# A three-block network on one core: statistics, blocks and one attention pair taken at other steps of the phase borders

## The chip, the core and the metric

The kernel runs on one core of one Trainium2 chip. The metric is the device time of one execution in microseconds: 2200.09 us is the median of three runs (2199.76 to 2200.43).

## What is computed

A sequence of 512 tokens of width 1024 goes through three mixers, each followed by a gated feed-forward network. All data is float32.

```python
# block 1: modulated (sh, sc, g come from a condition vector)
u = rms_norm(x, mix_pre_g) * (1 + sc1) + sh1
x = x + g1 * rms_norm(mix(u) @ w_out, mix_post_g)      # mix: mLSTM and a gated convolution
u = rms_norm(x, ffn_pre_g) * (1 + sc2) + sh2           # the "modulated norm"
x = x + g2 * rms_norm(ffn_conv(u), ffn_post_g)
# blocks 2 and 3: attention with forget gates ("fox"), a gated linear recurrence ("hgrn")
for mixer in (fox, hgrn):
    h = h + rmsnorm(mixer(rmsnorm(h, g0)), g1)
    h = h + rmsnorm(swiglu(rmsnorm(h, g2)), g3)
```

Five borders concern the change: the modulated norm (before the first network), and four plain ones (before fox, before the second network, before hgrn, before the third network). At each of them a projection ends, its output is normalised and added to the residual `X`, and the sum, normalised again, is the input `U` of the next phase.

## The kernel before

**Layout.** Everything lies transposed: 128 of the 1024 features on the partitions, 512 tokens along a row, so `X`, `U` and the projection's output `out.y` have 8 blocks (`KB`) each. The tokens fall into two halves of 256. A product of two float32 values is made of three: each operand is split into a high and a low part, and `mm3` (line 427) issues high by high, high by low and low by high, lines 430 to 432 of the profile. A weight unit's high part is a cast on ScalarE (line 155), its low part a subtraction on VectorE (line 157), both from `Weights.split`.

**Steps.** TensorE's order is the program's. Between products the program calls `slot()` (line 389), one *step*: it first runs evacuations that were posted and have waited out their lag, then resumes every generator in `sides` once (`rate` 1.0 at these borders). So a generator's `yield` says behind how many further products its next TensorE instruction stands. ScalarE, VectorE and GpSimd get their order from the compiler, which ranks by place in the program and by what is ready. Each engine then works through its own queue in that order. The last argument of a generator's `chain`, `hf`, is the half.

**A border.** `tail` (line 503; `tail_all`, line 518, at the modulated norm) computes the projection's last columns, first for the first half of the tokens, then for the second, and after each half appends `nxt.chain(out, hf)` to the sides. A chain takes the column sums of the squares over the partitions: `rms` (line 578) has four products with ones (line 562), a scaling on VectorE (line 584), a power on GpSimd (`rpow`, line 567); then `bcast` (line 570) lays the result along the partitions by two transposes (line 575).

- `Norm.chain` (line 218) then makes one block a step: `block` (line 236) updates `X` (`residual`, lines 1159 and 1160), writes the high and low parts of `U` (243, 244) and adds the new square (593, 594). When a half's eight blocks are made, `upto` (line 229) starts `pre` (line 249): its sums, and one step later its broadcast and a copy into `box["rb"]` (line 256). `U` is not yet multiplied by that second factor; each evacuation of the next phase multiplies by `rb`.
- `ModNorm.chain` (line 282) makes one residual block a step, waits three steps, takes the second sums, and copies their broadcast into `self.rb` (line 304). The blocks are normalised in `get` (line 307; lines 314, 319 and 320), two ahead of the product that needs them.

**The next phase.** `group_halves` (line 477) opens it: six accumulators at the networks and at hgrn, four (and the gate rows, `extra`) at fox; first all eight blocks of the first half of the tokens, then of the second. It calls `norm.get` for each block and a step after every 18 products (15 at fox), eight steps a half. The first four accumulators are the four banks of `mm`, the others lie in `ax` (four banks too). It ends with `norm.finish()` and posts the evacuations (line 1177 in a network, 1510 at hgrn). Then come full `unit`s of 24 products, one `mm` bank each; at fox `unit_tok`, whose first two token blocks lie in `ax`.

**Fox.** `fox_gate` leaves the cumulated gate rows in `self.C` (line 1338); the scores of a pair of heads need them (line 1370). `fox_pair` (line 1341) waits until its keys and `C` are there, then four more steps for pair 0 and two for the others. At most two sides run at once.

Of the kernel before, what the change touches and what calls it, by code (L numbers as in the profile page):

```python
# [19 lines left out]
KB = 8  # L20
# [189 lines left out]
class Norm:  # L210
# [6 lines left out]

    def chain(self, out, hf):
        k = self.k
        yield  # L220
        r = out.r(hf)
        yield
        self.out = out
        self.rb[hf] = k.bcast(r)
        while self.n[hf] < KB:
            yield
            self.upto(self.n[hf] + 1, hf)

    def upto(self, n, hf):
        while self.n[hf] < min(n, KB):  # L230
            self.block(self.n[hf], hf)
            self.n[hf] += 1
            if self.n[hf] == KB:
                self.k.sides.append(self.pre(hf))
# [24 lines left out]
    def get(self, kb, hf):  # L259
        k = self.k  # L260
        while hf not in self.rb:
            k.slot()
        self.upto(kb + 2, hf)
        return self.U[kb]
# [8 lines left out]
class ModNorm:  # L273
# [7 lines left out]

    def chain(self, out, hf):
        k, c = self.k, HALVES[hf]
        yield
        r = out.r(hf)
        yield
        rb = k.bcast(r)
        if self.ss is None:
            self.ss = k.blk("ss")
        for j in range(KB):  # L290
            x = k.X[j][:, c]
            k.residual(x, out.y[j][:, c], rb, self.g[:, j:j + 1])
            if j == KB - 1:
                last = k.tmp(shape=[128, 256])
                k.nc.scalar.activation(last, x, AF.Square)
            else:
                k.square_acc(self.ss[:, c], x, j == 0)
            yield
        for _ in range(3):
            yield  # L300
        r = k.rms(self.ss[:, c], D, [last])
        yield
        rb = k.tmp(shape=[128, 256])
        k.nc.scalar.copy(rb, k.bcast(r))
        self.rb[hf] = rb

    def get(self, kb, hf):
        k, c = self.k, HALVES[hf]
        while hf not in self.rb:
            k.slot()  # L310
        while self.n[hf] < min(kb + 2, KB):
            j = self.n[hf]
            t = k.tmp(shape=[128, 256])
            k.V.tensor_mul(t, k.X[j][:, c], self.rb[hf])
            if len(self.U) <= j:
                self.U.append((k.blk("U", F32R), k.blk("U", F32R)))
            hi, lo = self.U[j][0][:, c], self.U[j][1][:, c]
            for o in (hi, t):
                k.nc.scalar.activation(o, t, AF.Identity, scale=self.gain[:, j:j + 1], bias=self.shift[:, j:j + 1])  # L319
            k.V.tensor_sub(lo, t, hi.bitcast(F32))  # L320
            self.n[hf] += 1
        return self.U[kb]

    def finish(self):
        self.k.dump("x1", self.k.X)
# [23 lines left out]
class Kernel:  # L349
# [19 lines left out]
    def mm(self, shape=None):  # L369
        return self.pp.tile(shape or [128, T], F32, name="mm", tag="mm", bufs=4)  # L370
# [93 lines left out]
    def group(self, n, get, evacs, kb=KB, ahead=1):  # L464

        ws = [self.W.take(ahead=n - 1 + ahead if i == 0 else 0, load=i == 0) for i in range(n)]
        pss = [self.mm() for _ in range(n)]
        for k in range(kb):
            U = get(k)
            for (wh, wl), ps in zip(ws, pss):  # L470
                self.mm3(ps, (wh[:, k], wl[:, k]), U, k == 0, k == kb - 1)
            if k == kb - 1:
                for ps, ev in zip(pss, evacs):
                    self.post(lambda ps=ps, ev=ev: ev(ps), 0)
            self.slot()
# [27 lines left out]
    def tail(self, F, out, evac, nxt, done=4):  # L503
# [4 lines left out]
        for hf, c in enumerate(HALVES):  # L508
# [7 lines left out]
            self.sides.append(nxt.chain(out, hf))  # L516

    def tail_all(self, get, out, evac, nxt):

        ws = [self.W.take(ahead=3 if i == 0 else 0, load=i == 0) for i in range(4)]  # L520
# [820 lines left out]
    def fox_pair(self, p, qs, ks, V, O):  # L1341

        nc = self.nc
        mm = self.PE.matmul
        while p not in ks or getattr(self, "C", None) is None:
            yield
        for _ in range(4 if p == 0 else 2):
            yield
        q, (k, kl) = qs[p], ks[p]
        sel = [self.selc[b * 64:b * 64 + 64, 2 * p + b:2 * p + b + 1].to_broadcast([64, 128]) for b in range(2)]  # L1350
        e1 = self.blk("Q", shape=[128, 2, 256])
        e3, e2 = [self.tmp(), self.tmp()], [self.tmp(), self.tmp()]
        pr = [[e2[b][:, 384:], e1[:, b], e2[b][:, 0:384], e3[b]] for b in range(2)]
        sums = self.small([128, 2, 4], tag="sums")

        def logits(*tbs):
            L = [self.ax() for _ in range(2)]
            o, out = 0, []
            for tb in tbs:
                n = tb * 128  # L1360
                out.append([L[b][:, o:o + n + 128] for b in range(2)])
                o += n + 128
            for tb, o in zip(tbs, out):
                for b in range(2):
                    mm(o[b], q[b][:, tb * 128:tb * 128 + 128], k[b][:, :tb * 128 + 128], start=tb == tbs[0], stop=False)
            for tb, o in zip(tbs, out):
                for b in range(2):
                    hs = slice(b * 64, (b + 1) * 64)
                    mm(o[b], q[b][hs, tb * 128:tb * 128 + 128], kl[hs, :tb * 128 + 128], start=False, stop=False)
                    mm(o[b], sel[b], self.C[hs, :tb * 128 + 128], start=False, stop=False)  # L1370
            for tb, o in zip(tbs, out):
                for b in range(2):
                    mm(o[b][:, tb * 128:], self.identr, self.maskr, start=False, stop=tb == tbs[-1])
            return out

        def soft(tb, L):
            for b in range(2):
                e = pr[b][tb]
                mn = self.small([128, 1], tag="mn")
                self.V.tensor_reduce(out=mn, in_=L[b], axis=mybir.AxisListType.X, op=ALU.min)  # L1380
                nc.scalar.activation(e, L[b], AF.Exp, scale=-1.0, bias=mn, accum_out=sums[:, b, tb:tb + 1])

        L3 = logits(3)
        yield
        soft(3, L3[0])
        L2 = logits(2)
        yield
        soft(2, L2[0])
        L1 = logits(1, 0)
        yield  # L1390
        soft(1, L1[0])
        soft(0, L1[1])
        rs = self.small([128, 2, 4], tag="rs")
        self.V.reciprocal(rs, sums)
        for tb in (3, 2, 0, 1):
            for b in range(2):
                self.V.tensor_scalar(pr[b][tb], pr[b][tb], rs[:, b, tb:tb + 1], None, op0=ALU.mult)
        yield
        yield


        def trans(bank, b, *tbs):
            o = 0
            for tb in tbs:
                for sb in range(tb + 1):
                    self.PE.transpose(bank[:, o:o + 128], pr[b][tb][:, sb * 128:(sb + 1) * 128], self.ident)  # L1406
                    o += 128
            return bank

        T3 = [trans(self.ax(), b, 3) for b in range(2)]  # L1410
        yield
        nc.scalar.copy(e3[0], T3[0])
        self.V.tensor_copy(e3[1], T3[1])
        T2 = [trans(self.ax(), b, 2, 0) for b in range(2)]
        yield
        nc.scalar.copy(e2[0], T2[0])
        self.V.tensor_copy(e2[1], T2[1])
        T1 = self.ax([128, 2, 256])
        for b in range(2):
            trans(T1[:, b], b, 1)  # L1420
        yield
        nc.scalar.copy(e1, T1)
        yield
        po = self.ax()
        blocks = [(tb, sb) for tb in (3, 2, 0, 1) for sb in range(tb + 1)]
        for tb, sb in blocks:
            for b in range(2):
                h = 2 * p + b
                mm(po[b * 64:(b + 1) * 64, tb * 128:(tb + 1) * 128],  # L1429
                   V[sb][h // 8][:, (h % 8) * 64:(h % 8 + 1) * 64], pr[b][tb][:, sb * 128:(sb + 1) * 128],  # L1430
                   start=(tb, sb) == blocks[0], stop=(tb, sb) == blocks[-1])
        yield
        if self.dump_fn:
            t = self.tmp()
            nc.scalar.copy(t, po)
            self.dump("foxo%d" % p, [t])
        O[p] = self.hilo(po, "H")
# [309 lines left out]
```

## Time and profile before

| | |
|---|---|
| median of three runs | 2200.09 us |
| the profiled execution | 2198.21 us |
| its span, first to last instruction | 2196.5 us |
| mean granted TensorE clock | 0.991 of 2.4 GHz |

The rows below come from the profiled execution, with times from the start of its span. PE is TensorE, DVE VectorE, ACT ScalarE, POOL GpSimd. A wait is listed with the instruction that ended it.

### The profile page before, as it was taken

The numbers are of one execution on the slowest core, as the hardware profiler recorded it, in microseconds if no ns is written. First come the engines' busy times: TensorE is split into PE (matmuls) and PEld (weight loads), VectorE is DVE, ScalarE is ACT, GpSimd is POOL, SyncE is SP. The second block draws the span as 40 slices with busy tenths as digits, with TensorE's granted clock in tenths as the row PEclk, the third lists the DMA queues.
The fourth block names the chain that finished last, engine by engine and source line by source line (L and its number), as shares of the span: only waits on it lengthen the run. The fifth ranks groups of instructions, "written<-read, shape, count | busy, mean of one in ns | idle before, by whom it ended". The sixth has DMA issues, their size and how long they took to land.

```text
span 2196.5 us, 30266 instructions
## 1 busy us (share of the span) xinstructions
PE 2133.2 (97%) x12008; PEld 1836.7 (84%) x12008; DVE 1414.1 (64%) x2530; ACT 915.3 (42%) x1478; POOL 52.5 (2%) x82
## 2 busy tenths in 40 slices
PE   6999999989999999999999999999999999999997
PEld 5788887888888888888898888888899888888887
DVE  7899999877455557756575243457777837434445
ACT  4433343555343334655453222236566545232221
POOL 0000000000000000000000000000000000000000
PEclk8999999999999999999999999999999999999999
DMA  8332223613322221211123223222211112232321
GB/s 294 116 125 77 78 77 115 230 58 134 135 95 98 97 96 58 78 58 58 58 75 108 96 92 101 95 92 86 74 49 58 49 58 96 87 106 89 103 91 63
DMA packets 68109, 209.00 MB, mean 95 GB/s; under 512 B 7808, under 2 KB 9984, under 8 KB 67968
## 3 DMA queue, kind: packets, MB, share of 16 engines
q1 hardware_dynamic: 67968, 207.06, 27.5%
q8 instruction: 95, 1.56, 0.3%
q14 instruction: 46, 0.38, 0.1%
HBM read 204.94 MB, written 2.10 MB: 94 GB/s over the span
## 4 chain that ended last, share of the span: by engine, by line
PE 71%; DVE 4%; ACT 2%; issue 1%; POOL 0%; DMA 0%; POOLq 0%; DVEq 0%; ACTq 0%
PE mm L430 19%; PE mm L431 19%; PE mm L432 19%; PE ax L1600 2%; PE mm L456 1%; PE mm L457 1%; PE mm L458 1%; PE ax L1429 1%; PE ax L1406 1%; DVE wl L157 1%; PE ax L432 1%; DVE X L1160 1%; PE ax L430 1%; PE ax L431 1%; DVE ss L594 1%
## 5 line engine op out<-in xcount | busy, mean ns | idle before, releaser
L430 PE MATMUL mm<-U,wh 128*128 128x512 f32 (+1 forms) x1768 | 671.8, 380 | 4.1 <-ACT U L319 3.0
L432 PE MATMUL mm<-U,wl 128*128 128x512 f32 (+1 forms) x1768 | 659.2, 373 | 4.6 <-DVE wl L157 4.5
L431 PE MATMUL mm<-U,wh 128*128 128x512 f32 (+1 forms) x1768 | 658.7, 373 | 2.0 <-DVE U L320 2.0
L155 ACT CAST wh<-w 128x1024 fp32r<-128x1024 f32 (+1 forms) x325 | 335.6, 1035 | 749.2 <-PE mm L431 452.3
L157 DVE TENSOR_TENSOR wl<-w,wh 128x1024 fp32r<-128x1024 f32 (+1 forms) x325 | 389.8, 1202 | 210.4 <-ACT wh L155 196.7
L432 PEld LDWEIGHTS mm<-U,wl 128*128 128x128 f32 x1768 | 336.1, 190 | 65.2 <-DVE wl L157 7.4
L430 PEld LDWEIGHTS mm<-U,wh 128*128 128x128 f32 x1768 | 336.5, 190 | 64.2 <-ACT U L319 3.5
L431 PEld LDWEIGHTS mm<-U,wh 128*128 128x128 f32 x1768 | 336.6, 190 | 57.7 <-DVE U L320 2.4
L430 PE MATMUL mm<-H,wh 128*128 128x512 f32 (+1 forms) x868 | 310.0, 357 | 0.7 <-ACT H L599 0.7
L431 PE MATMUL mm<-H,wh 128*128 128x512 f32 (+1 forms) x868 | 307.0, 354 | 0.2 <-DVE H L600 0.2
L432 PE MATMUL mm<-H,wl 128*128 128x512 f32 (+1 forms) x868 | 307.0, 354 | 0.0
L430 PEld LDWEIGHTS mm<-H,wh 128*128 128x128 f32 x868 | 164.4, 189 | 23.4 <-ACT H L599 0.9
L431 PEld LDWEIGHTS mm<-H,wh 128*128 128x128 f32 x868 | 164.6, 190 | 23.1 <-DVE H L600 0.5
L432 PEld LDWEIGHTS mm<-H,wl 128*128 128x128 f32 x868 | 164.4, 189 | 22.8 <-DVE wl L157 0.2
L832 DVE SCALAR_TENSOR_TENSOR Y<-G,par,Y 128x504 f32<-128x504 f32 (+27 forms) x240 | 164.1, 729 | 0.5
L456 PE MATMUL mm<-wh,U 128*128 128x256 f32 x368 | 106.2, 289 | 0.0
L458 PE MATMUL mm<-wh,U 128*128 128x256 f32 x368 | 104.0, 283 | 0.0
L457 PE MATMUL mm<-wl,U 128*128 128x256 f32 x368 | 104.0, 283 | 0.0
L1197 DVE TENSOR_TENSOR Y<-Y,mm 128x512 f32<-128x512 f32 (+1 forms) x60 | 34.7, 580 | 106.6 <-PE mm L432 106.4
L1177 DVE TENSOR_TENSOR t<-mm,rb 128x512 f32<-128x512 f32 x42 | 29.0, 690 | 101.2 <-PE mm L432 101.2
L1187 DVE TENSOR_TENSOR t<-t,mm 128x512 f32<-128x512 f32 x42 | 28.7, 686 | 101.3 <-PE mm L432 101.3
L594 DVE TENSOR_TENSOR ss<-ss,t 128x256 f32<-128x256 f32 (+1 forms) x143 | 64.6, 458 | 26.5 <-ACT t L593 26.4
(360 smaller groups left out, 2730.0 us busy)
## 6 DMA issues: line engine op xcount, KB each, us to landing
w<-in_upa SPq DMA_DIRECT2D x44, 512.0 KB, 3.3
w<-in_upb SPq DMA_DIRECT2D x44, 512.0 KB, 3.3
w<-in_upc SPq DMA_DIRECT2D x44, 512.0 KB, 3.3
H<-in_ada SPq DMA_DIRECT2D x48, 256.0 KB, 5.8
w<-in_wglu SPq DMA_DIRECT2D x16, 512.0 KB, 4.4
w<-in_wqk SPq DMA_DIRECT2D x16, 512.0 KB, 3.2
U<-in_ada SPq DMA_DIRECT2D x32, 256.0 KB, 6.1
w<-in_wfqk SPq DMA_DIRECT2D x16, 512.0 KB, 3.3
```

The costliest lines, as they stand in the source:

```text
L155: nc.scalar.copy(wh, raw)
L157: k.V.tensor_sub(wl, raw, wh.bitcast(F32))
L430: mm(ps, lh, rh, start=start, stop=False)
L431: mm(ps, lh, rl, start=False, stop=False)
L432: mm(ps, ll, rh, start=False, stop=stop)
L456: mm(ps, lh, wh[:, k % 4], start=k == 0, stop=False)
L457: mm(ps, lh, wl[:, k % 4], start=False, stop=False)
L458: mm(ps, ll, wh[:, k % 4], start=False, stop=k == 7)
L594: self.V.tensor_add(ss, ss, sq)
L832: self.V.scalar_tensor_tensor(y[:, s:], G[j][:, :T - s], cvw[:, w:w + 1], y[:, s:], op0=ALU.mult, op1=ALU.add)
L1197: self.V.tensor_add(acc[m][:, c], acc[m][:, c], ps[:, c])
L1600: mm(ps[:, ts], W[:, ts], W[:, ts], start=True, stop=True)
```

## The change

`Norm.chain` lets two more steps pass for the second half before its first column sums. `ModNorm.chain` lets one more pass for the second half, makes two residual blocks a step, and after the second broadcast normalises four blocks on its own, one a step; the loop that did this in `get` is now `upto`. Pair 0 of the attention lets six steps pass instead of four.

```diff
--- before.py
+++ after.py
@@ -217,7 +217,8 @@
 
     def chain(self, out, hf):
         k = self.k
-        yield
+        for _ in range(3 if hf else 1):
+            yield
         r = out.r(hf)
         yield
         self.out = out
@@ -281,7 +282,8 @@
 
     def chain(self, out, hf):
         k, c = self.k, HALVES[hf]
-        yield
+        for _ in range(2 if hf else 1):
+            yield
         r = out.r(hf)
         yield
         rb = k.bcast(r)
@@ -295,7 +297,8 @@
                 k.nc.scalar.activation(last, x, AF.Square)
             else:
                 k.square_acc(self.ss[:, c], x, j == 0)
-            yield
+            if j % 2:
+                yield
         for _ in range(3):
             yield
         r = k.rms(self.ss[:, c], D, [last])
@@ -303,12 +306,19 @@
         rb = k.tmp(shape=[128, 256])
         k.nc.scalar.copy(rb, k.bcast(r))
         self.rb[hf] = rb
+        while self.n[hf] < 4:
+            yield
+            self.upto(self.n[hf] + 1, hf)
 
     def get(self, kb, hf):
+        while hf not in self.rb:
+            self.k.slot()
+        self.upto(kb + 2, hf)
+        return self.U[kb]
+
+    def upto(self, n, hf):
         k, c = self.k, HALVES[hf]
-        while hf not in self.rb:
-            k.slot()
-        while self.n[hf] < min(kb + 2, KB):
+        while self.n[hf] < min(n, KB):
             j = self.n[hf]
             t = k.tmp(shape=[128, 256])
             k.V.tensor_mul(t, k.X[j][:, c], self.rb[hf])
@@ -319,7 +329,6 @@
                 k.nc.scalar.activation(o, t, AF.Identity, scale=self.gain[:, j:j + 1], bias=self.shift[:, j:j + 1])
             k.V.tensor_sub(lo, t, hi.bitcast(F32))
             self.n[hf] += 1
-        return self.U[kb]
 
     def finish(self):
         self.k.dump("x1", self.k.X)
@@ -1344,7 +1353,7 @@
         mm = self.PE.matmul
         while p not in ks or getattr(self, "C", None) is None:
             yield
-        for _ in range(4 if p == 0 else 2):
+        for _ in range(6 if p == 0 else 2):
             yield
         q, (k, kl) = qs[p], ks[p]
         sel = [self.selc[b * 64:b * 64 + 64, 2 * p + b:2 * p + b + 1].to_broadcast([64, 128]) for b in range(2)]
```

## Rows read from the trace of the kernel before

**Rows 1.** The page of the profile: its first line, and the busy time of each engine with its share of the span and its instructions.

```profile
span 2196.5 us, 30266 instructions
PE 2133.2 (97%) x12008; PEld 1836.7 (84%) x12008; DVE 1414.1 (64%) x2530; ACT 915.3 (42%) x1478; POOL 52.5 (2%) x82
```

**Rows 2.** What TensorE (PE) waited for in the whole span: the waiting instruction by tile and line, what released it, us in total, times, the longest.

```profile
PE ax L562 <- DVE ss L594: 8.2, 7, 2.2
PE ax L575 <- POOL r L567: 7.4, 8, 1.9
PE mm L430 <- ACT U L319: 3.0, 2, 1.6
PE mm L431 <- DVE U L320: 2.0, 2, 1.3
PE ax L1370 <- DVE Q L1338: 2.3, 2, 2.1
```

**Rows 3.** TensorE in order of time, around the modulated norm and once before it: start us, duration us, engine, line, operation, out<-in, shapes, count, and in brackets the engine's idle time before it and what ended it.

```profile
369.52 0.70 PE L1117 MATMUL ax<-ss,ones 128*128 128x512 f32 x1 [4.09 <-DVE ss L840]
457.45 0.68 PE L562 MATMUL ax<-ones,ss 128*128 128x128 f32 x4 [1.32 <-DVE ss L594]
458.67 0.36 PE L430 MATMUL mm<-G,H 128*128 128x256 f32 x1
460.18 0.38 PE L575 MATMUL ax<-ident,r 128*128 128x128 f32 x2
463.46 0.38 PE L430 MATMUL mm<-U,wh 128*128 128x256 f32 x1 [1.48 <-ACT U L319]
464.55 0.39 PE L431 MATMUL mm<-U,wh 128*128 128x256 f32 x1 [0.71 <-DVE U L320]
486.94 0.43 PE L575 MATMUL ax<-ident,r 128*128 128x128 f32 x2 [1.09 <-POOL r L567]
488.93 0.39 PE L430 MATMUL mm<-U,wh 128*128 128x256 f32 x1 [1.55 <-ACT U L319]
490.64 0.58 PE L431 MATMUL mm<-U,wh 128*128 128x256 f32 x1 [1.33 <-DVE U L320]
```

**Rows 4.** Busy time by stretch (us from the span's start): length, then busy us and instructions in it of PE, PEld (weight loads), DVE, ACT and POOL, then the granted TensorE clock as a share of 2.4 GHz, the DMA share and GB/s.

```profile
370.30:373.60 3.30, 3.30 (x8) 2.32 (x7) 3.27 (x10) 0.83 (x2) 0.00 (x0) 0.50 0.00 0
440.35:457.30 16.95, 15.78 (x132) 15.57 (x130) 15.98 (x38) 8.96 (x17) 0.00 (x0) 1.00 0.43 156
465.85:469.20 3.35, 3.35 (x18) 3.35 (x17) 1.27 (x3) 2.63 (x5) 0.00 (x0) 0.50 0.00 0
473.34:484.58 11.24, 11.00 (x92) 10.83 (x91) 10.54 (x28) 6.05 (x13) 0.00 (x0) 1.00 0.01 1
491.20:496.50 5.30, 5.30 (x27) 5.30 (x26) 2.39 (x7) 5.05 (x11) 0.00 (x0) 0.50 0.00 0
874.30:889.90 15.60, 15.60 (x132) 15.60 (x131) 13.53 (x21) 13.05 (x20) 0.00 (x0) 1.00 0.40 133
1129.90:1144.80 14.90, 14.90 (x127) 14.90 (x126) 8.75 (x23) 5.17 (x13) 0.00 (x0) 1.00 0.00 1
```

**Rows 5.** Groups of instructions on VectorE (DVE) from 440 to 462 us: line, engine, operation, out<-in, shapes, count, busy us, mean ns of one, idle before.

```profile
L157 DVE TENSOR_TENSOR wl<-w,wh 128x1024 fp32r<-128x1024 f32 x4 | 4.9, 1223 | 1.1 <-ACT wh L155 1.0
L594 DVE TENSOR_TENSOR ss<-ss,t 128x256 f32<-128x256 f32 x12 | 4.8, 419 | 0.3 <-ACT t L593 0.2
L935 DVE TENSOR_TENSOR Q<-Q,mm 128x256 f32<-128x256 f32 x6 | 2.5, 413 | 0.2 <-PE mm L432 0.2
```

**Rows 6.** The fox border and the attention in order of time, TensorE and VectorE; columns as in rows 3.

```profile
845.89 0.68 PE L562 MATMUL ax<-ones,ss 128*128 128x128 f32 x4 [2.22 <-DVE ss L594]
852.97 0.42 DVE L594 TENSOR_TENSOR ss<-ss,t 128x256 f32<-128x256 f32 x1
853.53 0.68 PE L562 MATMUL ax<-ones,ss 128*128 128x128 f32 x4 [1.41 <-DVE ss L594]
890.03 0.63 PE L1365 MATMUL ax<-Y 128*128 128x512 f32 x2
893.19 0.50 PE L1370 MATMUL ax<-Q,selc 64*128 64x512 f32 x1 [2.10 <-DVE Q L1338]
898.84 0.63 PE L1365 MATMUL ax<-Y 128*128 128x512 f32 x2
```

**Rows 7.** Where a phase takes over `rb` and its first full unit starts, in order of time, at the second feed-forward network (1147 to 1152), at the recurrence (1520) and at the third network (1853); columns as in rows 3.

```profile
1147.48 0.38 PE L575 MATMUL ax<-ident,r 128*128 128x128 f32 x2
1148.53 0.36 ACT L256 COPY rb<-ax 128x256 f32<-128x256 f32 x1
1149.84 0.68 DVE L1177 TENSOR_TENSOR t<-mm,rb 128x512 f32<-128x512 f32 x1
1152.01 0.40 PE L430 MATMUL mm<-U,wh 128*128 128x512 f32 x1
1520.37 0.68 DVE L1510 TENSOR_TENSOR t<-mm,rb 128x512 f32<-128x512 f32 x1
1853.19 0.68 DVE L1177 TENSOR_TENSOR t<-mm,rb 128x512 f32<-128x512 f32 x1
```

**Rows 8.** GpSimd (POOL), the reciprocal root between the sum of 457.45 and its broadcast; columns as in rows 3.

```profile
459.19 0.82 POOL L567 TENSOR_TENSOR r<-v,neghalf 128x2 f32<-128x2 f32 x1 [19.55 <-DVE v L584]
```

## The prediction

> **What bounds the kernel now.** I began with the busy shares: TensorE is busy for 97% of the span [rows 1], so a change of order can only win TensorE's idle time, or lose some more. Next, the list of what TensorE waited for [rows 2]: column sums that wait for a running sum of squares (8.2 us in 7 waits), broadcasts that wait for `r` from GpSimd (7.4 in 8), first products that wait for a normalised block (3.0 and 2.0), and one pair's gate rows (2.3). Then TensorE in order of time, to place them [rows 3]. At the modulated border it waits 1.32 us at 457.45, then 1.48 and 0.71 when the feed-forward phase opens, then 1.09, 1.55 and 1.33 before that phase's second half. The stretches [rows 4] add what such waits bring after them: granted clock 0.50, the 1.2 GHz level, at 465.85 to 469.20 and at 491.20 to 496.50, where 27 products took 5.30 us, 0.20 each, instead of 0.12. At the fox border there are waits of 2.22 and 1.41, and a wait of 2.10 in the attention [rows 6].
>
> A "step" below is one call of `slot()`, which resumes each side generator once. Steps lie between TensorE instructions, whose order is fixed by hand, so moving a TensorE instruction by a step moves it past all products of that step. No moved part issues a DMA.
>
> **Column sums of the second half, four plain borders.** `Norm.chain` for the second half starts with the next phase, which has 16 steps (8 a half). Now: sums at step 2, broadcast at 3, one block a step from 4 to 11. The block loop then starts `pre`: its sums at step 13, its broadcast and the copy to `rb` at step 14. Counting products confirms it: about 126, seven steps of 18, between `pre`'s first and second turn [rows 4]. After the change all of it is two steps later: `pre`'s sums at 15, broadcast at 16, behind the phase's last product.
>
> What it gains: only the fox border has a wait at that first sum, 2.22 us at 845.89. I give it nothing. Three steps on stands the other half's `pre` sum, which waits until VectorE has added its eighth block, issued at 852.97 [rows 6]; that chain of blocks needs nothing from the moved instruction. TensorE would come 2.22 earlier and wait 1.41 + 2.22 there. At the other three borders this sum waits for nothing.
>
> What it costs: every evacuation of the phase multiplies by `rb`, and the six accumulators hold all four `mm` banks. Today `rb` is copied at 1148.53, the first evacuation runs at 1149.84 and the next unit starts at 1152.01 without a wait; at 1520.37 and 1853.19 it is the same [rows 7]. Afterwards the transposes are issued at 1152.01 themselves: 0.38 transposes, 0.36 copy, 0.68 multiplication, some 0.15 of handovers, less 0.12 in which TensorE still issues: **1.45 us** in which the unit's 24 products, and through them the release of weight buffers to the casts and loads behind, stand still. At three borders with six accumulators: **+4.35**. Below: 1.3 each, without handovers. Above: a cast on ScalarE or a 1.22 us split on VectorE [rows 5] ahead in the queue, so 2.7 each. At the fox border it costs nothing: the first two token blocks write the other bank set, 48 products or some 5.7 us at the pace of rows 4, against a delay of two steps of 15 products (3.6). Nor do the 1.41 or the like at `pre`'s first turn change.
>
> **Modulated norm, first half.** One block a step becomes two, so the second sum goes from step 14 to step 10 of the sixteen of the projection's second half: 48 products of 0.12 earlier, 5.8 us, reached at 450.3 instead of 456.1 [rows 3, 4]. Does the residual chain finish by then? VectorE spent 440.35 to 457.30 on it at 94% busy [rows 4]. An instruction of this kind occupies 0.38 us (28 in 10.54 [rows 4]): eight blocks of multiply, update and add 9.0, the four evacuations that fall due meanwhile 1.5, three splits of 1.22 [rows 5] 3.7: 440.35 + 14.2 = **454.5**. Between ends: 450.9 if the splits let the blocks pass, 457.3 if nothing gets quicker. I take 454.5 because the same eight blocks in the other half, with few strangers between, still took 11.24 us [rows 4]. So TensorE waits 4.2 us there, where it waited 1.32; behind it in its queue stand 72 products of the projection and the whole next phase. From the sum's start the restart takes 1.22 [rows 3], 72 products 8.76, the broadcast 0.15: the phase opens at 464.6. Four blocks are normalised by then (five steps, 7.3 us), so 1.48 and 0.71 are gone; but the present opening, counted back from the second product at 464.55 [rows 3], is 464.43. **+0.2**.
>
> The clock: after 4.09 us of waiting at 369.52 the granted clock was 0.50 from 370.3 to 373.6 [rows 3, 4]; after the lone 1.32 it did not fall. At 4.2 us I take the fall, by the nearer row: 3.3 us in which a product takes 0.20 or 0.21 instead of 0.12 lose about **+1.4**. (Ends: 0, and 1.7, half of it.)
>
> The broadcast behind that sum waits for `r`: GpSimd took 0.82 us and ended 0.17 before the broadcast began [rows 3, 8]. I keep that, so nothing is added. The Trainium skill, SBUF — State Buffer, section "SBUF: two separate sides", says that VectorE and GpSimd share a port pair as an exclusive lock, so that a GpSimd instruction waits for a whole VectorE instruction with two SBUF inputs. By that rule the busier VectorE could add up to about 0.5 to this sum, an estimate; rows 8 show no such wait.
>
> **Modulated norm, second half.** From the phase's opening to the first product of its second half that ran on (490.64 [rows 3]) are 26.2 us: broadcast, eight blocks at VectorE's pace, sums, `r`, broadcast, first normalised block. The first sum goes one step later (+2.2), the slow stretch at the opening goes (3.35 us, -1.5), one normalised block fewer sits among the residuals (-0.7): **0**. The blocks normalised ahead don't help here: `rb` comes at step 12, the half's products end at step 8. The slow stretch from 491.20 stays.
>
> **First pair later.** The 2.10 us wait is not this pair's. The first scores at 890.03 stand 132 products, 11 steps, after the projection [rows 4]. Both pairs enter at step 9; pair 1 waits two steps (11), pair 0 four (13, its scores at 898.84 [rows 6], where TensorE waits for nothing). Six steps put pair 0 at 15, and pair 1 waits as before: **0**. Ends: -2.3 if I have the pairs the wrong way round; +1 if pair 0 then collides with the evacuations of the next pair.
>
> **Sum:** 4.35 + 0.2 + 1.4 + 0 = 5.95. The profiled execution took 2198.21 us (span 2196.5), so 2204.2; the median of the runs lies 1.88 above it, so **2206.0**.
>
> **Rivals.** *A, the residuals make it (not slower).* If VectorE's sum is done by about 451, TensorE waits under 1 us at step 10, the clock holds and the phase opens at 461.1: -3.3 for this border, in all +1.05, **2201.1**. For it: the splits are of use only to the next phase. Against: they slipped in between today's blocks too. The point is 453; before it the border gains, after it it loses. *B, the fox wait is won and `rb` is in time (faster).* Then 4.35 falls away, 3.6 is won at the fox border and 3.3 at the modulated one: **2193.2**. Against: the step count, and the add at 852.97. It needs `pre`'s broadcast before step 15. *C, a longer bank wait.* A cast and a split ahead of copy and multiplication at each border: three times 3.0 instead of 1.45, **2210.7**. For it: ScalarE was casting right around 1148.53 [rows 7]. *D, nothing acts:* if the compiler's order on VectorE hides every move, 2200.1.
>
> **How the numbers follow.** Forecast 0.48, A 0.22, B 0.07, C 0.15, D and unknown ripples 0.08. A measurement of this kernel tells about 0.2%, 4.4 us, from no change. Forecast: 2204 to 2208, mostly above 2204.5, about 0.40 slower and 0.08 same; C 0.15 slower; A same but for 0.01; B 0.02 same, 0.05 faster; the rest splits 0.02 slower, 0.02 same, 0.04 faster: slower 0.57, same 0.33, faster 0.10. The range reaches down past A (to 2199, with pair 0 or the sum better than thought) and up to C, 2199 to 2211; the forecast's own range is 2203.5 to 2208.5.
>
> **What would show it.** In the profile after: `r` in the plain borders' second turn right before the next unit, and a wait of about 1.45 us of `mm` products on the `rb` multiplications (lines 1177 and 1510 of before) at three borders; at the fox border no 2.22 but about 3.6 at the next sum; at the modulated border one wait of about 4 us where 1.32, 1.48 and 0.71 were; the 2.10 unchanged. No bank wait at the three borders, or a sum ready before 452, would make me wrong.

## The result, and the profile after

The changed kernel took **2223.07 us** (2220.32 to 2224.03, four runs) against 2199.93 for the kernel before in the same session (2198.52 to 2200.43): ratio 1.0100, 95% interval 1.0088 to 1.0112, 23 us slower. The prediction said 2206.0, with 2199 to 2211 as the range: the sign was right, the size a quarter of the real one. The profiled execution took 2222.6 us. Here and below, a ratio is to runs of the kernel before in the same session.

The page after, to be read against [rows 1]:

```profile
span 2220.8 us, 30252 instructions
PE 2145.5 (97%) x12008; PEld 1845.8 (83%) x12008; DVE 1414.8 (64%) x2530; ACT 916.1 (41%) x1478; POOL 52.8 (2%) x82
```

The span grew by 24.3, TensorE's busy time by 12.3, with the same 12008 instructions. So about half of the loss is new waiting, and the other half is products that took longer. The list of waits (these line numbers are larger by 9: sums 571, broadcast 584, products 439 to 441, evacuations 1186 and 1519), to be read against [rows 2]:

```profile
PE ax L571 <- DVE ss L603: 11.8, 6, 4.5
...
PE mm L439 <- DVE t L1186: 5.2, 2, 2.7
PE ax L1379 <- DVE Q L1347: 3.1, 1, 3.1
PE mm L439 <- DVE t L1519: 2.5, 1, 2.5
```

The two lines with `t` are new: they are the bank waits. Sums that wait for `ss` rose from 8.2 to 11.8. TensorE in order of time puts each in its place (as in [rows 3, 6, 7]; instructions that waited, and the broadcast of 1136.55):

```profile
454.77 0.55 PE L571 MATMUL ax<-ones,ss 128*128 128x128 f32 x1 [4.52 <-DVE ss L603]
491.41 0.38 PE L439 MATMUL mm<-U,wh 128*128 128x256 f32 x1 [1.61 <-ACT U L329]
855.93 0.35 PE L571 MATMUL ax<-ones,ss 128*128 128x128 f32 x1 [2.00 <-DVE ss L603]
878.68 0.32 PE L584 MATMUL ax<-ident,r 128*128 128x128 f32 x1 [0.59 <-POOL r L576]
898.94 0.79 PE L1379 MATMUL ax<-Q,selc 64*128 64x512 f32 x1 [3.10 <-DVE Q L1347]
...
1136.55 0.38 PE L584 MATMUL ax<-ident,r 128*128 128x128 f32 x2
1138.17 0.38 PE L571 MATMUL ax<-ones,ss 128*128 128x128 f32 x1 [1.25 <-DVE ss L603]
1166.14 0.47 PE L439 MATMUL mm<-U,wh 128*128 128x512 f32 x1 [2.65 <-DVE t L1186]
1513.81 0.38 PE L571 MATMUL ax<-ones,ss 128*128 128x128 f32 x1 [1.24 <-DVE ss L603]
1541.60 0.47 PE L439 MATMUL mm<-U,wh 128*128 128x512 f32 x1 [2.48 <-DVE t L1519]
1849.90 0.38 PE L571 MATMUL ax<-ones,ss 128*128 128x128 f32 x1 [1.25 <-DVE ss L603]
1877.73 0.64 PE L439 MATMUL mm<-U,wh 128*128 128x512 f32 x1 [2.51 <-DVE t L1186]
```

Each of the three later borders now has two waits of its own: 1.25 at the first half's sum for the next `r` (0.66, 0.10 and 0.73 before), and 2.5 to 2.65 at the first full unit (none before). The first of these sums in the kernel before:

```profile
1126.87 0.71 PE L562 MATMUL ax<-ones,ss 128*128 128x128 f32 x4 [0.66 <-DVE ss L594]
```

Where the time went is read best from stretches that hold the same products in both kernels. First the kernel before (columns as in [rows 4]; the clock is the third number from the end): modulated border, fox border, first part of the attention, border of the second feed-forward network, of the recurrence, of the third network, and 4 us behind that.

```profile
410.31:510.49 100.18, 91.15 (x705) 88.80 (x704) 69.09 (x176) 45.77 (x89) 2.91 (x4) 0.95 0.31 110
817.88:874.19 56.31, 52.13 (x433) 50.32 (x432) 40.07 (x92) 25.32 (x51) 2.96 (x4) 1.00 0.13 48
874.19:945.34 71.15, 68.83 (x507) 59.24 (x505) 49.80 (x88) 46.03 (x96) 0.00 (x0) 1.00 0.24 82
1087.98:1152.01 64.03, 61.55 (x506) 60.49 (x505) 41.60 (x90) 32.40 (x66) 2.96 (x4) 1.00 0.25 84
1459.39:1522.52 63.13, 59.98 (x481) 58.98 (x480) 44.33 (x99) 29.39 (x58) 2.96 (x4) 0.97 0.21 70
1791.33:1855.35 64.02, 61.48 (x505) 60.46 (x504) 41.56 (x90) 31.11 (x65) 2.89 (x4) 1.00 0.25 85
1855.35:1859.35 4.00, 4.00 (x20) 3.31 (x19) 3.36 (x7) 2.62 (x4) 0.00 (x0) 1.00 0.61 228
```

The same stretches of the changed kernel:

```profile
410.18:512.89 102.71, 92.48 (x705) 90.03 (x704) 68.92 (x176) 45.97 (x89) 2.92 (x4) 0.93 0.30 108
820.28:878.87 58.59, 54.48 (x433) 51.56 (x432) 40.85 (x92) 25.02 (x50) 2.97 (x4) 0.97 0.16 53
878.87:953.50 74.63, 71.53 (x506) 61.20 (x506) 49.12 (x88) 46.53 (x96) 0.00 (x0) 0.95 0.22 72
1096.12:1166.14 70.02, 64.30 (x506) 63.03 (x504) 42.57 (x91) 32.94 (x67) 2.96 (x4) 0.95 0.27 90
1473.60:1541.60 68.00, 61.22 (x482) 59.98 (x480) 45.32 (x99) 29.79 (x58) 2.95 (x4) 0.95 0.23 78
1810.53:1877.73 67.20, 61.63 (x505) 60.36 (x504) 42.54 (x91) 31.68 (x66) 2.89 (x4) 1.00 0.29 93
1877.73:1881.73 4.00, 4.00 (x11) 3.18 (x12) 3.90 (x7) 2.30 (x4) 0.00 (x0) 0.57 0.46 147
```

The lengths differ by +2.5, +2.3, +3.5, +6.0, +4.9 and +3.2; behind the last wait the next phase loses 1.7 more, for the clock was 0.57 there and 11 instructions fitted where 20 did. The phases between the borders take as long as before, within 0.2 us. From the fox border to the end, first the kernel before, then the changed one:

```profile
817.88:2196.49 1378.61, 1346.03 (x8061) 1178.69 (x8059) 787.13 (x1434) 576.19 (x981) 24.14 (x26) 1.00 0.23 79
820.28:2220.80 1400.52, 1357.13 (x8061) 1186.79 (x8059) 787.75 (x1434) 576.90 (x981) 24.36 (x26) 0.99 0.23 78
```

There the same 8061 instructions keep TensorE busy 11.1 us longer, and it is idle 10.8 us longer.

### The profile page after: what moved, and what is told of

Same layout as the page of the kernel before. It is cut to its first block, busy times and chain, and to the rows that moved or that the text cites. A ratio compares the mean times of both kernels' runs of the same rounds, so it can differ in the third digit from the quotient of the medians.

```text
span 2220.8 us, 30252 instructions
## 1 busy us (share of the span) xinstructions
PE 2145.5 (97%) x12008; PEld 1845.8 (83%) x12008; DVE 1414.8 (64%) x2530; ACT 916.1 (41%) x1478; POOL 52.8 (2%) x82
## 4 chain that ended last, share of the span: by engine, by line
PE 71%; DVE 3%; ACT 2%; issue 1%; DMA 0%; POOL 0%; POOLq 0%; DVEq 0%; ACTq 0%
PE mm L439 19%; PE mm L440 19%; PE mm L441 19%; PE ax L1609 2%; PE mm L465 1%; PE mm L466 1%; PE mm L467 1%; DVE wl L157 1%; PE ax L1438 1%; PE ax L1415 1%; ACT wh L155 1%; PE ax L441 1%; PE ax L440 1%; PE ax L439 1%; PE ax L1382 0%
## 5 line engine op out<-in xcount | busy, mean ns | idle before, releaser
L439 PEld LDWEIGHTS mm<-H,wh 128*128 128x128 f32 x868 | 164.4, 189 | 23.7 <-ACT H L608 0.9
```

The source lines that it names most:

```text
L439: mm(ps, lh, rh, start=start, stop=False)
```

## Experiments

Two theories stood against each other after this reading. **Queues:** the plain norm's two steps make two waits a border, one on VectorE's queue and one on the banks, and each brings a stretch at half rate (granted clock 0.50, the 1.2 GHz level) behind it. **Elsewhere:** the modulated norm or the pair, or the mere lateness of the sums, causes it.

**One part at a time: sums.**

```
 class Norm, chain(out, hf), kernel before:
-        yield
+        for _ in range(3 if hf else 1):
+            yield
         r = out.r(hf)
```

> The kernel before with the later column sums in the four plain norms alone; modulated norm and attention pair as before. Theory (reading of the changed trace): the loss sits at the plain borders, namely bank waits of 2.5 to 2.65 us at the three borders with six accumulators, half-rate stretches behind waits at the fox border, in the attention and at two of the three, so 20 to 22 of the 23 us appear here: about 2221 us. The prediction's own sum for this part is 4.35 us: about 2204 us. Rival: the modulated norm shifts the rest of the kernel and so makes the later waits; then this kernel loses less than 10 us.

Measured: 2219.52 us, ratio 1.0085 (1.0071 to 1.0099), 18.7 us. The plain norms carry nearly all of it; the prediction had 4.35 for them. With the two parts below, the ratios of the three parts alone add up to 1.0088, at the lower end of the interval of the whole.

**The modulated norm alone** (the diff's `ModNorm` part on the kernel before).

> The kernel before with the modulated norm's part alone (two residual blocks a step, later sums of the second half, blocks normalised ahead). Theory: the modulated border costs what the changed trace shows there, 2.4 to 2.5 us, and nothing behind it changes: about 2202.5 us, with one wait of about 4.5 us at its first-half sum. The prediction's sum for this part is 1.6 us: 2201.6. Rival: the shift of 2.5 us alone disturbs later borders, 5 us or more.

Measured: 1.0006 (0.9997 to 1.0014), 1.3 us, which neither refutes 1.6 nor 2.5; 5 us is excluded. The 4.5 us wait was there.

**The pair alone** (`range(6 if p == 0 else 2)` on the kernel before).

> The kernel before with the first attention pair two steps later and nothing else. Theory: the 2.10 us wait belongs to the second pair, so nothing changes: within 0.5 us of before. Rival 1: the wait is the first pair's and goes: 2.3 us faster. Rival 2: the later pair meets the evacuations and costs 1 us or more.

Measured: 0.9997 (0.9989 to 1.0006); the wait of 2.10 is still there. No effect, as predicted.

**Late sums without the late `rb`.** The changed kernel, with the second half's blocks two at a time until four are done:

```
         while self.n[hf] < KB:
             yield
-            self.upto(self.n[hf] + 1, hf)
+            self.upto(self.n[hf] + (2 if hf and self.n[hf] < 4 else 1), hf)
```

> The changed kernel with the second half's plain blocks made at two a step in their first two steps, so that the column sums and the residuals still begin two steps later, while the second half's last blocks, the sum for the next r, its broadcast and the copy to rb come at the steps that they had before the change. Theory: the bank waits of 2.5 us at the three borders with six accumulators go, and with them the half-rate stretches behind them; what stays is the modulated border's 2.5 us: 2201 to 2206 us. Rival: the later column sums or the denser VectorE cost by themselves, and the time stays above 2213 us.

Measured: 2210.64, ratio 1.0044 (1.0029 to 1.0060). The three bank waits are gone, the gate's wait is 2.10 again, and the first units start without a wait, so the late `rb` and what follows it cost 1.0100 less 1.0044, about 12 us. But the time lies between the two expectations: with the modulated norm's 1.0006 taken off, something else in the plain norms costs 0.0038, some 8 us. The waits of 1.25 stayed, and this is where they come from. VectorE's queue in the changed kernel, up to the sum of 1138.17:

```profile
1134.60 0.16 DVE L593 TENSOR_SCALAR v<-ax 128x2 f32<-128x2 f32 x1 [2.84 <-PE ax L571]
1134.68 0.41 DVE L1168 TENSOR_TENSOR t<-Y,ax 128x256 f32<-128x256 f32 x1
...
1136.96 0.42 DVE L1168 TENSOR_TENSOR t<-Y,ax 128x256 f32<-128x256 f32 x1 [0.75 <-PE ax L584]
1137.30 0.48 DVE L245 SCALAR_TENSOR_TENSOR U<-X,par,U 128x256 fp32r<-128x256 f32 x1
1137.70 0.42 DVE L603 TENSOR_TENSOR ss<-ss,t 128x256 f32<-128x256 f32 x1
```

Two strangers stand in the queue among the first half's last blocks. `v` (1134.60) reads the moved sums; VectorE stood still for 2.84 us until TensorE came to them. The multiplication at 1136.96 is the second half's first block; it needs the moved broadcast, which TensorE began at 1136.55. Only behind it come the first half's last split and its last add to `ss` (1137.70), and for that add TensorE waits at 1138.17: it issues the broadcast and goes straight on to the sum, while VectorE needs three more instructions, 1.2 us. Before the change the same `v` came without a stop. The wait was 1.24 to 1.25 at the three later borders of every kernel with this order, whether the stop at `v` was 2.84 or, in the kernel with the sums alone, 0.18: it is the broadcast that sets it. (One border of the kernel with four weight buffers, below, where `v` came without a stop, had 1.84.) The Trainium skill, TensorE: Matmul & The Clock Gate, section "Architectural detail: the array is 16× 32×32, not 1× 128×128", says that the queues of ScalarE and VectorE are strictly first in, first out; these rows agree: the add needs neither the sums nor the broadcast, and stands still behind both.

These waits are not the 8 us, though. From the fox border on, the kernel with `pre` kept is idle only 1.8 us longer than the kernel before; its products take 7.9 us longer. No half-rate stretch follows a wait of 1.24 or 1.25 in any profile. At the three later borders of this kernel the stretches begin some 12 us ahead of it, at the border's opening. Here is the second network's, and the same place in the kernel before, where 27 products fit instead of 15:

```profile
1123.30:1126.50 3.20, 3.20 (x15) 3.20 (x16) 3.20 (x8) 1.63 (x4) 0.00 (x0) 0.50 0.57 210
1116.20:1119.40 3.20, 3.20 (x27) 3.15 (x28) 3.20 (x8) 1.63 (x4) 0.00 (x0) 1.00 0.51 161
```

**Take the sum out of the way as well.** The previous kernel, and `pre` of the first half two steps later:

```
     def pre(self, hf):
-        yield
+        for _ in range(1 if hf else 3):
+            yield
```

> The kernel of e4_pre_kept with one more edit: the first half's sum for the next r stands two steps later in the four plain norms. In e4_pre_kept VectorE stood still for 1.63 us at 1132.45, because the reading of the late column sums stands in its queue ahead of the first half's last residual blocks, and TensorE then waited 1.24 for that half's sum at 1136.02. Theory: VectorE's stop stays, but with TensorE two steps later at that sum the waits of 1.24, 1.25, 1.24 and 2.00 us go and with them the half-rate stretches behind them: 2202 to 2206 us. Rival: the stretches come from the waits of the borders' opening, or the late sums cost by themselves; then at most 4 us come back and the time stays above 2207.

Measured: 2202.16, ratio 1.0006 (0.9997 to 1.0015). The waits of 1.25 went, and so did the 2.00 of the fox border, where instead the second half's next sum now waits 1.84 (869.23), with no stretch behind it. The borders of the second network, 63.00 us with full clock against 64.03 before, and of the recurrence:

```profile
1090.70:1153.70 63.00, 61.18 (x506) 60.37 (x504) 41.62 (x90) 32.34 (x66) 2.79 (x4) 1.00 0.28 86
1461.08:1524.69 63.61, 60.55 (x481) 59.76 (x480) 44.37 (x99) 29.38 (x58) 2.79 (x4) 0.95 0.22 69
```

All column sums of the second half are still two steps late here, and the time is back at that of the kernel before. That doesn't show that their lateness costs nothing in itself: the last edit also takes away waits that the kernel before has (1.41, 0.66, 0.10 and 0.73), and on that kernel, together with a later second pair, it gains 3.3 us (below). What is shown is the price of each part: 0.0056 for the late `rb`, 0.0038 for the late sums with `rb` in time, 0.0006 for the modulated norm, together 0.0100, in us 12.3, 8.4 and 1.3, the first two to about 4 us either way. Between the profiles of the last two kernels, from the fox border on, the waits differ by 3.6 us (25.5 and 21.9, added over TensorE's rows) and the time by 9.6; the rest is the clock.

**Why the bank wait is 2.6 and not 1.45.** The changed kernel at the second network's border:

```profile
1163.09 1.04 ACT L155 CAST wh<-w 128x1024 fp32r<-128x1024 f32 x1 [2.52 <-DMA w<-in_upb]
1163.10 0.38 PE L584 MATMUL ax<-ident,r 128*128 128x128 f32 x2
1164.04 0.36 ACT L257 COPY rb<-ax 128x256 f32<-128x256 f32 x1
1164.17 1.23 DVE L157 TENSOR_TENSOR wl<-w,wh 128x1024 fp32r<-128x1024 f32 x1 [2.17 <-ACT wh L155]
1165.31 1.28 DVE L1186 TENSOR_TENSOR t<-mm,rb 128x512 f32<-128x512 f32 x2
```

The broadcast ends at 1163.48. Ahead of the copy to `rb` stands a cast whose weight has just landed (copy at 1164.04, 0.56 late), and ahead of the multiplication the split of that cast (0.9 late). A fourth buffer lets that weight come earlier:

```
-  "w": 3
+  "w": 4
-  "ss": 3
+  "ss": 2
```

> The changed kernel with four buffers instead of three for raw weights (and two instead of three for sums of squares, which pays for the room). In the changed kernel a cast that waits for a weight's load stands in ScalarE's queue ahead of the copy to rb, and its split stands in VectorE's queue ahead of the multiplication. Theory: with a fourth buffer the load is there in time, the cast and the split are done before the broadcast, and the bank waits shrink from 2.65, 2.48 and 2.51 us to about 1.4 each; 3 to 4 us faster than the changed kernel, about 2219.5. Rival: the wait is set by something else in the queues and stays at 2.5 us: about 2223.

Measured: 2218.31, ratio 1.0075 (1.0058 to 1.0093) against 1.0100. The bank wait fell to 1.28 at all three borders, just under the 1.45 of the prediction, with 0.47 for `r` ahead of it:

```profile
1158.14 1.61 POOL L576 TENSOR_TENSOR r<-v,neghalf 128x2 f32<-128x2 f32 x1 [21.98 <-DVE v L593]
...
1159.80 0.32 PE L584 MATMUL ax<-ident,r 128*128 128x128 f32 x1 [0.47 <-POOL r L576]
...
1161.51 0.49 PE L439 MATMUL mm<-U,wh 128*128 128x512 f32 x1 [1.28 <-DVE t L1186]
```

So cast and split were worth 1.2 to 1.4 us of each bank wait, and the wait for `r` took 0.5 of that back. (The run also has one buffer fewer for sums of squares; what that does alone was not measured.) By the time alone the two intervals are not quite apart; the waits are.

**Half the distance.** `range(2 if hf else 1)` in `Norm.chain` of the kernel before.

> The kernel before with the second half's column sums in the four plain norms one step later instead of two. Theory: the waits come from a chain that is late by steps of some 2.2 us against a fixed need, so they fall by more than half: the bank waits of 2.5 us become 0.3 (the copy to rb comes a whole step of 18 products earlier), VectorE's stop at the late sums is shorter by 2.2 us and the first half's next sum waits as before; 1 to 4 us slower than before, 2201.5 to 2204.5. Rival: each step costs the same, half of the 18 us that two steps cost: about 2209.5.

Measured: 2209.13, ratio 1.0035 (1.0021 to 1.0049), about 8 us. The sum of the waits came out near the theory: no bank wait, and 0.40 to 0.47 for the 1.25 at the three later borders, though 2.71 at the fox border; added in the same way they are 25.0 us (23.7 before, 34.6 after the change). The time did not. The products were slower, here at the fox border and at the third network's:

```profile
820.13:878.80 58.67, 54.14 (x433) 51.59 (x432) 40.96 (x93) 25.21 (x51) 3.95 (x4) 0.97 0.16 54
1800.80:1866.60 65.80, 63.16 (x505) 61.93 (x504) 42.10 (x91) 31.44 (x66) 3.81 (x4) 0.97 0.27 86
```

The last border waited 0.1 us more than before and took 1.8 longer. My theory of waits alone fails here; what differs is the granted clock. From the fox border on, the products take 8.5 us longer than before and the waits 1.2. So a kernel without the bank wait and without the 1.25 loses as much as the one with `pre` kept: late sums bring slower products, in part at least, by a way other than these two waits.

**The clock, twice.** Both kernels once more, unaltered.

> The changed kernel once more, unaltered, for a second profile. Theory: the waits are set by the order of the queues and return within 0.1 us (4.5 at the modulated border, 2.00, 0.6 and 3.1 at the fox border and in the attention, 1.25 and 2.5 at each later border); the half-rate stretches behind them vary, by up to 1.5 us at a border. Rival: the stretches are as fixed as the waits.

> The kernel before once more, unaltered, for a second profile. Theory: the same waits within 0.1 us; half-rate stretches that the first profile lacked at the attention, the ffn b border and the hgrn border (1.5, 0.7 and 0.7 us in the kernels that leave these places unaltered) can show up, so that single profiles of before differ by 1 to 3 us there. Rival: the stretches stand where the first profile had them.

Measured: 2222.18 and 2198.38. The kernel before repeated its profile within 0.15 us at every border, half-rate stretches included, as the rival has it. But both of its profiles have a mean granted clock of 0.991, and so have only 13 of its 62 runs in the three sessions of the experiments (their median is 2198.3 us); 36 have 0.988 or less and take up to 2206.1. So its stretches do vary, and its two profiles show the kernel with few of them. The changed kernel repeated its waits within 0.15, and its total, but not the places of its stretches. The border of the second network, 70.02 in the first profile, and the 4 us behind the third:

```profile
1096.23:1163.45 67.22, 61.64 (x505) 60.37 (x504) 42.60 (x91) 33.04 (x67) 2.96 (x4) 1.00 0.28 94
1877.42:1881.42 4.00, 4.00 (x11) 3.17 (x12) 3.90 (x7) 2.32 (x4) 0.00 (x0) 0.57 0.44 135
```

The granted clock in slices of 0.5 us gives this count of half-rate time (us in slices below 0.95) at the plain borders and in the attention's first part, "behind" being the first unit after a border:

| kernel | fox | attention | 2nd net, behind | recurrence, behind | 3rd net, behind | sum |
|---|---|---|---|---|---|---|
| before, twice | 0 | 0 | 0, 0 | 3.5 to 4, 0 | 0, 0 | 3.5 to 4 |
| modulated norm alone | 4 | 4 | 0, 0 | 7, 0 | 0, 0 | 15 |
| pair alone | 0 | 4 | 3.5, 0 | 7, 0 | 0, 0 | 14.5 |
| changed | 3.5 | 7.5 | 7.5, 0 | 7.5, 0 | 0, 4 | 30 |
| changed, again | 4 | 7 | 0, 3.5 | 4, 4 | 0, 3.5 | 26 |
| sums alone | 4 | 7 | 0, 3.5 | 4, 4 | 0, 3.5 | 26 |
| `pre` kept | 4 | 7.5 | 3.5, 0 | 4, 0 | 4, 0 | 23 |
| `pre` kept, sum later | 0 | 4 | 0, 0 | 7.5, 0 | 0, 0 | 11.5 |
| changed, four buffers | 4 | 7 | 4, 4 | 7.5, 0 | 0, 0 | 26.5 |
| one step | 4 | 7 | 4, 0 | 4, 0 | 4, 0 | 23 |

What it shows: a stretch behind a border is there only where a bank wait ended it, after seven of the nine waits of about 2.5 us or more (the two without one had 7.5 us at the border's opening) and after one of the three waits of 1.28. At the fox border a stretch follows the sum in all six profiles in which it waits for 2.0 to 2.7 us; the 2.22 or 2.23 that the sum of the kernel before waits there brought one in the modulated norm alone and in the last kernel below, and none in five other profiles, two of them of the kernel before. And the rows of the modulated norm alone and the pair alone, whose plain borders are those of the kernel before, have some 15 us where its two profiles have 3.5 to 4: part of the difference in this table is not the change's. What it doesn't show is why the same opening waits (0.21, 0.49, 0.15, 0.96 at the networks) bring a stretch in one kernel and none in another. That stays open.

**Towards a faster kernel.** The waits that the trace named can be moved from without late sums: `pre` of the first half two steps later as above, on the kernel before, and the second pair two steps later.

```
-        for _ in range(4 if p == 0 else 2):
+        for _ in range(4 if p < 2 else 2):
```

> The kernel before with the first half's sum for the next r two steps later in the four plain norms and the second attention pair two steps later; column sums of the second half as before. Theory: TensorE's waits of 1.41 us (fox border), 0.66, 0.10 and 0.73 for that sum go, and so does the 2.10 us wait for gate rows, which is the second pair's: 4 to 6 us faster than before, 2194 to 2197. Rival: the waits only move, to the broadcast behind that sum and to a later pair: within 1.5 us of before.

Measured: 2197.26, ratio 0.9985 (0.9976 to 0.9994). The waits of 1.41, 0.66, 0.10, 0.73 and 2.10 are gone, which shows that the 2.10 was the second pair's; 1.47 and 1.22 appear in the pairs' transposes, where one of 0.5 was, and take part of it back. Less than expected, but faster.

In the modulated norm, the changed code with the sum two steps later (`range(5)` for `range(3)` ahead of `rms`):

> The kernel before with the modulated norm's part alone, but with five steps instead of three between the last residual blocks and the sum, so that the first half's sum stands at step 12 of 16 instead of 10 (14 in the kernel before). Theory: VectorE has the sum ready at about 454.6 us as in the changed kernel and TensorE reaches it at about 454.7, so the 4.5 us wait goes, and the blocks normalised ahead take away the two waits at the phase's opening (1.48 and 0.71) with the half-rate stretch behind them: 3 to 6 us faster than before, about 2196. Rival: VectorE's queue holds the sum back again (its evacuations and splits come first), and the time is within 1.5 us of before.

Measured: 2199.33, ratio 0.9996 (0.9987 to 1.0004): 0.9 us, which can't be told from none. In its profile the modulated border took 96.77 us for 100.18, with one wait of 1.70 where the 1.32, 1.48 and 0.71 of [rows 3] were; the second and third networks' borders were slower by their clock (64.66 at the third, 64.02 before, with fewer waits).

Both together:

> The kernel before with the edits of e6_pre0_pair1 and of e7_mod_two_later together: two residual blocks a step in the modulated norm with its first sum at step 12, the first half's next sum two steps later in the plain norms, the second pair two steps later. The two act at different borders. Theory: the gains add, 3.3 and 1.4 us on the medians: 2195 to 2197, faster than both kernels. Rival: half-rate stretches move elsewhere and eat one of them: 2198 to 2200.

Measured: **2194.46 us**, ratio 0.9972 (0.9963 to 0.9982), 6 us faster than the kernel before and 28 faster than the change. The modulated border (100.18 before) and the second network's (64.03 before):

```profile
410.93:507.47 96.54, 89.28 (x705) 86.66 (x704) 68.78 (x176) 45.76 (x89) 3.02 (x4) 0.96 0.32 114
1084.23:1147.32 63.09, 61.27 (x505) 60.41 (x504) 41.62 (x90) 32.28 (x66) 2.78 (x4) 1.00 0.27 86
```

## Why the prediction was wrong, step by step

**The steps held.** The second half's `pre` sums stood at step 15 and its broadcast (1163.10) behind the phase's last product, as counted; bank waits came at the three borders with six accumulators and not at the fox border; the 2.22 of the fox border went and came back further on.

**The step that failed** is in the column sums: "that chain of blocks needs nothing from the moved instruction", and "Nor do the 1.41 or the like at `pre`'s first turn change". By data that is so. By the queue it is not: `v` and the second half's first block, which need the moved TensorE instructions, stand in VectorE's queue ahead of the blocks on which the next sum depends. I looked at what the moved instruction needs and not at what is queued behind its readers. The waits show it: the 0.66, 0.10 and 0.73 became 1.25, 1.24 and 1.25, while at the fox border 2.00 of the predicted 3.6 remained, behind which the clock fell. Price of the late sums 0, measured 8.4 us (with `rb` in time). Of this, waits are the smaller part, 1.8 us in all from the fox border on; the rest is slower products: half of that kernel's half-rate time stands at the later borders' openings, a third in the attention, and what brings it is open.

**A term mis-sized:** the bank wait, 1.45 each. Without the cast and the split it is 1.28, so the sum of durations was right; with them 2.48 to 2.65. Rival C had the mechanism (with 3.0), and I gave it 0.15, although a cast stood right around 1148.53 [rows 7]. The nearer question was what stands ahead of the copy in its queue: a cast that waited for its load. The gate's 2.10 that I left unchanged became 3.10 for the same late `rb`; with `pre` kept it is 2.10.

**A term left out:** the clock. I priced a fall at the modulated border alone, by the 4.09 of [rows 3], and it came there. At the other borders I added waits of 1.45 and no fall, by the lone 1.32. Half of the 24 us is this: from the fox border to the end waits rose by 10.9 us (23.7 to 34.6), and the time by 21.9. The late `rb`, with bank waits, gate and stretches, cost 12.3 against 4.35. Both profiles compared here are single ones, and that of before is one with few stretches.

**Right:** the modulated norm (+1.6 predicted, sum ready at 454.5 against 454.6 measured, 1.3 us measured alone, which can't be told from none; in the two profiles of the changed kernel its border took 2.5 and 1.2 us longer, and the half-rate stretch behind its wait lasted over 6 us, not the 3.3 of the prediction), the second half's slow stretch that stays (1.61 at 491.41), the pair (0). "Rows 8 show no such wait" was read too quickly: `r` took 0.82 there and 0.70 at 438.94, where VectorE ran nothing. At the modulated sum the changed kernel has 0.83, so the estimate of up to 0.5 more came to 0.1. Had I taken 2.6 for the bank wait and one stretch behind each, 7.8 and 5, the sum would have been some 2215. The last 8 are the late sums' own price, of which VectorE's queue explains the waits.

## What to carry to other kernels

When a TensorE instruction is moved later, list its readers on the other engines and then everything that stands behind those readers in their queues; that, not the data flow, says who waits. A new wait of TensorE is to be priced with the half-rate stretch that can follow it, here some 1.4 to 1.7 us behind seven of nine waits of 2.5 us (behind a wait of 2.22 or 2.23, two of seven). Two profiles that agree don't show that a kernel's stretches are fixed: compare the granted clock of all runs. And where TensorE waits at a sum or a broadcast whose result is needed much later, moving that instruction alone is cheap and can gain.

## What was not expected of the hardware

GpSimd's `r` took 1.60 to 1.61 us at the three borders with a fourth weight buffer, where VectorE's split of 1.22 had begun 0.16 earlier (1157.98 against 1158.14), and 0.69 at the same place in the changed kernel, without a split beside it. The Trainium skill, SBUF — State Buffer, section "SBUF: two separate sides", says that VectorE, with two SBUF inputs, and GpSimd share a port pair that one holds for its whole instruction; here the traces agree, and what it added was 0.9 us, of which TensorE waited 0.47. The kernel before had it too, outside the rows that the prediction read: an `r` of 128x4 took 1.92 us beside such a split (1587.02), and 1.01 at 1751.22, where VectorE ran nothing:

```profile
1587.18 1.92 POOL L567 TENSOR_TENSOR r<-v,neghalf 128x4 f32<-128x4 f32 x1 [70.11 <-DVE v L584]
```

The granted clock is no smooth cost: two kernels with the same waits at a border, 2.54 and 2.64 us in all, took 64.02 and 65.80 there.
